# One run of products through both halves of a channel mixer, with the second half's operands prepared early and kept in DRAM

## The chip, the cores and the metric

The kernel runs on one core of a Trainium2 chip. The metric is the device time of one execution in microseconds (us). The core has TensorE (PE: matrix products, from SBUF into PSUM), VectorE (DVE), ScalarE (ACT) and GpSimd (POOL) for elementwise work, and SyncE (SP), whose queue issues nearly all transfers of this kernel. Each engine takes its instructions in order.

## What is computed

The reference is one encoder block on x of 2048 positions by 1024 channels. The change touches the second sub-layer alone, the channel mixer:

```python
h = rms_norm(x, g_pre_ffn[l]) * (1.0 + sc_f) + sh_f
y = conv_ffn(h, w_up[l], w_dw_ffn[l], b_dw_ffn[l], w_down[l])
x = x + gt_f * rms_norm(y, g_post_ffn[l])

def conv_ffn(h, w_up, w_dw, b_dw, w_down):
    u = causal_dwconv(h @ w_up, w_dw, b_dw)      # width 3 over positions
    val, gt = jnp.split(u, 2, axis=-1)           # 2 x 2816 channels
    return (jax.nn.gelu(gt) * val) @ w_down
```

## The kernel before

Data lie channels by positions, in tiles of 128 channels by 512 positions. Numbers are kept accurate by splitting each operand in a high and a low part: a product of two operands is three matmuls (high-high, low-high, high-low).

The channel mixer works in two halves of 1024 positions. A half is a loop of 22 **stages**, one for each block of 128 value channels and 128 gate channels (`n`, `NJ = 22`). The up-projection of a stage is a 2x2 block product in seven products instead of eight: seven **token terms** (B11, T2, T1, B21, T3, T4, B22), which are sums and differences of blocks of h, meet seven weight factors (A11, S2, S1, A12, S3, A22, S4), which are sums and differences of blocks of `w_up`. `sprod` (L1179) issues one such product, 12 matmuls at L1188. The token terms (28 pairs of tiles, two f16 parts each) are made once for each half by `h2prep` (L1119): it loads x from DRAM (`XD`), scales it (L1129), and forms and splits the terms on VectorE and ScalarE. They stay in SBUF for the whole half, in the pool `fh`, which has room for one half's terms.

The weights of each stage are loaded (`upload`, two 512 KB loads to the tile `wst`, of which there are three), combined (`combine`), and split with a power-of-two scale `sw` (`pairV`, `pairA`, `pairB`, `pair4`, all through `wpair`, L288 on ScalarE and L289 on VectorE). The scale comes from the weights' squares: `upsquare` (ScalarE, L259), then `uptable` (L1098), which is a small matmul (L1104), about six small VectorE instructions (L219 to L224) to the power of two, and three more. Squares and tables are made in the first half only; the second half finds `sw` in SBUF.

The order of one stage n, as TensorE sees it, is: on odd n above 2, first the down-projection `down` of the two gated blocks before it (96 matmuls, L1263 to L1265); A11 of n; A22 and S4 of n-1; S2 of n; then, in the first half, the small matmul of `uptable(n+1)`; S1, A12 and S3 of n. `order` chains all of these in the order of the program. `pairV(n+1)`, which makes the weights of the next stage's first product, stands behind A12 of n, and `ready(n+1)` (the loads and squares of the next weights) behind A11 of n. Between the products the results are taken from PSUM to the rows `ub`, convolved (`taps3`, L1241 to L1247), multiplied (L1405) and split into `gh` and `gl`, the operands of `down`, whose results VectorE adds to `y2` (L1273).

Other work is hung under the products with a generator, `under`: each `sprod` takes one step of it. In the first half it is `post(NB - 1)`, the rest of the sub-layer before; in the second half it is `finals` of the first half (mean square, scale, residual, store). Between the halves stands, not hung under anything:

```python
        dw[NG - 1] = [dchunk(C_DN + 4 * (NG - 1) + q) for q in range(4)]
        if half == 0:
            down(NG - 1)
            h2prep(1)
            under = finals()
        else:
            down_final()
```

`dchunk` loads a 256 KB piece of `w_down` into a tile `xt` (four of them in all, which `h2prep` and `finals` use too) and splits it into `whi` and `wlo`. `tc.high_priority(offset=...)` tells the scheduler to place instructions as if they stood that many instructions earlier in the program; a tile that is asked for again is given out when its last reader is done.

The functions that the change touches:

Of the kernel before, what the change touches and what calls it, by code (L numbers as in the profile page):

```python
# [78 lines left out]
def hybrid_block_kernel(ctx: ExitStack, tc: tile.TileContext, xT, vec, bvrow, band, wada, wall, outT):  # L79
# [1007 lines left out]
    hb = {}  # L1087

# [24 lines left out]

    def htile(x, i):
        t = fh.tile([P, 2, 512], F16, name=f"{x}_{i}")
        hb[x, i] = t[:, 0, :], t[:, 1, :]
        return hb[x, i]

    def h2prep(half):  # L1119

        ta = fa.tile([P, 2, 512], F32, name="ta", tag="t0", bufs=1)
        tb = fa.tile([P, 2, 512], F32, name="tb", tag="t1", bufs=1)
        for i in range(4):
            x = {}
            for q, bb in ((0, 0), (0, 1), (1, 1), (1, 0)):
                k = 4 * q + i
                xt = mx.tile([P, 512], F32, name="xt", tag="xt", bufs=4)
                SY.dma_start(out=xt, in_=XD[2 * half + bb][k])
                V.scalar_tensor_tensor(out=xt, in0=xt, scalar=fsc[:, k:k + 1], in1=r2k[2 * half + bb], op0=ALU.mult, op1=ALU.mult)  # L1129
                x[q, bb] = xt  # L1130

# [3 lines left out]
            def direct(name, q, bb):  # L1135
                hi, lo = htile(name, i)
                A.activation(hi, x[q, bb], AF.Identity, bias=shift(q))
                V.scalar_tensor_tensor(out=lo, in0=x[q, bb], scalar=shift(q), in1=hi, op0=ALU.add, op1=ALU.subtract)

            def summed(name, t):  # L1140
                hi, lo = htile(name, i)
                A.activation(hi, t, AF.Identity)
                V.tensor_tensor(out=lo, in0=t, in1=hi, op=ALU.subtract)

            t1, t3, t2, t4 = ta[:, 0, :], ta[:, 1, :], tb[:, 0, :], tb[:, 1, :]
            direct("B11", 0, 0)
# [3 lines left out]
            summed("T2", t2)  # L1150
            summed("T1", t1)
            V.scalar_tensor_tensor(out=t3, in0=x[1, 1], scalar=shift(1), in1=x[0, 1], op0=ALU.add, op1=ALU.subtract)
            direct("B21", 1, 0)
            summed("T3", t3)
            V.scalar_tensor_tensor(out=t4, in0=x[1, 0], scalar=shift(1), in1=t2, op0=ALU.add, op1=ALU.subtract)
            summed("T4", t4)
            direct("B22", 1, 1)
# [13 lines left out]
    h2prep(0)  # L1171
    NG = NJ // 2
    under = post(NB - 1)
# [19 lines left out]
    for half in range(2):  # L1193
        y2, W, U, gt, stg, sums = {}, {}, {}, {}, {}, {}

        def pairs(st, j, tag):

            t = m1.tile([P, 2, 1024], F16, name="up", tag=tag)
            wpair(st, U_UP + 2 * j, (t[:, 0, :], t[:, 1, :]))
            return [(t[:, 0, c:c + 512], t[:, 1, c:c + 512]) for c in (0, 512)]  # L1200

        def combine(j, st, half=half):

            a, g = st
            if j == 0 and half == 0:
                s12 = wp.tile([P, 1024], F32, name="wst", tag="wst", bufs=3)
            else:
                s12 = fr.tile([P, 1024], F32, name="s12", tag="r2k0")
            s4 = fa.tile([P, 512], F32, name="s4", tag="s4", bufs=1)
            s2, s1 = s12[:, 0:512], s12[:, 512:1024]  # L1210
            V.tensor_tensor(out=s1, in0=g[:, 0:512], in1=g[:, 512:1024], op=ALU.add)
            V.tensor_tensor(out=s2, in0=s1, in1=a[:, 0:512], op=ALU.subtract)
            V.tensor_tensor(out=g[:, 0:512], in0=a[:, 0:512], in1=g[:, 0:512], op=ALU.subtract)
            V.tensor_tensor(out=s4, in0=a[:, 512:1024], in1=s2, op=ALU.subtract)  # L1214
            return s12, s4

        def pairV(j):
            W["A11", j], W["A12", j] = pairs(stg[j][0], j, f"yl{j % 2}")

        def pairA(j):  # L1220
            W["S2", j], W["S1", j] = pairs(sums[j][0], j, "yl2")

        def pairB(j):
            W["S3", j], W["A22", j] = pairs(stg[j][1], j, "yl3")

        def pair4(j):
            t = fa.tile([P, 2, 512], F16, name="up4", tag="up4", bufs=1)
            W["S4", j] = t[:, 0, :], t[:, 1, :]
            wpair(sums[j][1], U_UP + 2 * j, W["S4", j])

        def urow(j, part):

            r = fa.tile([P, 1026], F32, name="ub", tag=f"u{part}", bufs=2 - part)
            G.tensor_copy(r[:, 0:2], carry[:, part * NJ + j, :])  # L1234
            return r

        def taps3(j, part, half=half):
            fi, r = part * NJ + j, U.pop((j, part))
            t = fa.tile([P, 1024], F32, name=f"t{part}", tag=f"t{part}", bufs=1)
            f = fws[:, j, part, :]  # L1240
            A.activation(t, r[:, 2:1026], AF.Identity, scale=f[:, 2:3], bias=col("fb", fi))  # L1241
            if half == 0:
                G.tensor_copy(carry[:, fi, :], r[:, 1024:1026])
            V.scalar_tensor_tensor(out=t, in0=r[:, 1:1025], scalar=f[:, 1:2], in1=t, op0=ALU.mult, op1=ALU.add)  # L1244
            V.scalar_tensor_tensor(out=t, in0=r[:, 0:1024], scalar=f[:, 0:1], in1=t, op0=ALU.mult, op1=ALU.add)  # L1245
            if part:
                A.activation(t, t, AF.Gelu_apprx_tanh)  # L1247
            return t

        def down(g, last=False):  # L1250
            w = dw.pop(g)
            for q in range(4):
                wh, wl = w[q]
                for mm in range(2):
                    m = 2 * q + mm
                    for bb in range(2):
                        ps = pr2.tile([P, 512], F32, name="mx")
                        c = slice(bb * 512, (bb + 1) * 512)
                        mms = []
                        for jj in range(2):  # L1260
                            gh, gl = gt[2 * g + jj]
                            a, b = [x[:, (2 * mm + jj) * P:(2 * mm + jj + 1) * P] for x in (wh, wl)]
                            mms.append(T.matmul(ps, a, gh[:, c], start=jj == 0, stop=False))  # L1263
                            T.matmul(ps, b, gh[:, c], start=False, stop=False)  # L1264
                            mms.append(T.matmul(ps, a, gl[:, c], start=False, stop=jj == 1))  # L1265
                        order(mms[0], mms[-1])
                        with tc.high_priority(offset=WPRI // 4):
                            if g == 0:
                                y2[m, bb] = m1.tile([P, 512], F32, name=f"y2_{m}_{bb}", tag=f"{('ym', 'yh')[bb]}{m}")
                                A.activation(y2[m, bb], ps, AF.Identity)  # L1270
                            else:
                                y = y2[m, bb]
                                V.tensor_tensor(out=y, in0=y, in1=ps, op=ALU.add)  # L1273

        def dchunk(i):

            with tc.high_priority(offset=WPRI):
# [15 lines left out]
        def finish(bb, c0, c1, ps, xt, last, half=half, y2=y2):  # L1293
            b = 2 * half + bb
            with tc.high_priority(offset=WPRI):
                r = rstd(ps, mx, 1, after=last, n=c1 - c0)
# [214 lines left out]
```

## Time and profile before

| | us |
|---|---|
| median of 3 runs (2994.25 to 2995.7) | 2994.99 |
| the profiled execution | 2989.23 |
| its span | 2987.4 |
| first-half stages, two and one `down`, from 1922.33 | 64.84 |
| second-half stages, two and one `down`, from 2418.78 | 59.32 |
| last S3 of the first half to the end of the first `down` of the second, 2199.81 to 2359.46 | 159.65 |

The profile times each instruction of one execution from the start of its span. The channel mixer runs from about 1493 us on to the end. Matmuls are pipelined: a row's length of a product (2.75 us for 12 matmuls) overlaps the next one's, and the distance from start to start is what counts. The stretches of the table are cut where TensorE ends a `down` and starts the next A11; 2199.81 is where the last S3 of the first half would be followed by the next product.

### The profile page before, as it was taken

To read this page: it belongs to the slowest core of one execution; us is meant where nothing else is said; L and a number is where in the kernel's file an instruction comes from. 1 tells how busy PE (TensorE), PEld (TensorE's weight loads), DVE (VectorE), ACT (ScalarE), POOL (GpSimd) and SP (SyncE) were. 2 spreads that over 40 slices of the span, in tenths; PEclk is the share of its full clock that TensorE was granted. 3 is DMA by queue.
4 is the path that set the end of the run, shared out by engine and by line. 5 is a ranking of instruction groups with operands and counts; after the bars stand their busy time and mean duration, and the time that the engine had idled before them with its cause. 6 is when DMAs were issued, how large, how long until landed. Compare 5 with 4: busy or idle time off the path is not lost. (4 is left out here: it accounts for less than half of the span.)

```text
span 2987.4 us, 38687 instructions
## 1 busy us (share of the span) xinstructions
PE 2776.3 (93%) x14286; PEld 1616.5 (54%) x14286; DVE 2282.7 (76%) x3360; ACT 1427.9 (48%) x2210; POOL 385.8 (13%) x387
## 2 busy tenths in 40 slices
PE   7999999999899999999879999999986899999996
PEld 3576666654344446556625555555552556556654
DVE  7858677669999575876986766777799677777776
ACT  5745766632312455555666334444455533443344
POOL 2102222200000002221201000101124000000002
PEclk8999999999999999999989999999998999999998
DMA  8657665531312466655641111111124311211121
GB/s 290 202 153 211 200 189 176 170 94 50 106 60 95 166 193 188 215 188 150 190 133 43 54 43 44 49 50 58 52 64 137 93 51 52 61 57 47 53 70 58
DMA packets 221215, 340.17 MB, mean 114 GB/s; under 512 B 52832, under 2 KB 69344, under 8 KB 221024
## 3 DMA queue, kind: packets, MB, share of 16 engines
q1 hardware_dynamic: 221024, 337.68, 36.6%
q8 instruction: 112, 1.84, 0.3%
q14 instruction: 79, 0.65, 0.1%
HBM read 268.40 MB, written 69.21 MB: 113 GB/s over the span
## 5 line engine op out<-in xcount | busy, mean ns | idle before, releaser
L1188 PEld LDWEIGHTS <-up 128*128 128x128 f16 x3696 | 364.8, 100 | 516.5 <-issue 65.2
L1188 PE MATMUL g<-T,up 128*128 128x512 f16 x1584 | 365.8, 381 | 4.0 <-DVE up L289 1.8
L402 PE MATMUL g<-hh,whi 128*128 128x512 f16 x768 | 295.4, 385 | 6.5 <-ACT whi L288 4.2
L1273 DVE TENSOR_TENSOR y<-y,mx 128x512 f32<-128x512 f32 x304 | 207.5, 685 | 120.3 <-PE mx L1265 117.8
L404 PE MATMUL g<-hh,whi 128*128 128x512 f16 x768 | 292.4, 383 | 2.4 <-DVE hh L364 2.0
L403 PE MATMUL g<-hh,wlo 128*128 128x512 f16 x768 | 293.4, 383 | 0.0
L1263 PE MATMUL mx<-gh,whi 128*128 128x512 f32 x672 | 273.3, 407 | 12.2 <-ACT gh L325 10.5
L846 DVE SCALAR_TENSOR_TENSOR a<-ut,vc,a 128x2048 f32<-128x2048 f32 x120 | 279.6, 2348 | 2.1
L1265 PE MATMUL mx<-gl,whi 128*128 128x512 f32 x672 | 269.4, 401 | 8.9 <-DVE gl L326 8.8
L1264 PE MATMUL mx<-gh,wlo 128*128 128x512 f32 x672 | 267.7, 398 | 8.3 <-DVE wlo L326 8.3
L289 DVE SCALAR_TENSOR_TENSOR up<-wst,sw,up 128x1024 f16<-128x1024 f32 x89 | 113.9, 1280 | 151.7 <-ACT up L288 151.7
L1188 PE MATMUL g<-B,up 128*128 128x512 f16 x528 | 141.2, 419 | 48.8 <-DVE up L289 19.9
L1234 POOL COPY ub<-carry 128x2 f32<-128x2 f32 x88 | 97.1, 1105 | 657.1 <-DVE t L1245 560.2
L1263 PEld LDWEIGHTS mx<-gh,whi 128*128 128x128 f32 x672 | 127.5, 190 | 49.7 <-ACT gh L325 15.5
L1265 PEld LDWEIGHTS mx<-gl,whi 128*128 128x128 f32 x672 | 127.3, 189 | 47.3 <-DVE gl L326 17.5
L325 ACT ACTIVATE whi<-xt 128x512 fp32r<-128x512 f32 x88 | 53.9, 625 | 204.8 <-PE mx L1265 203.7
L717 ACT ACTIVATE sx<-sx,st 128x640 f32<-128x640 f32 (+4 forms) x128 | 97.4, 761 | 109.6 <-DVE st L715 88.4
L1264 PEld LDWEIGHTS mx<-gh,wlo 128*128 128x128 f32 x672 | 127.6, 190 | 38.3 <-DVE wlo L326 8.7
L720 DVE SCALAR_TENSOR_TENSOR ph<-sx,ph 128x640 f16<-128x640 f32 (+4 forms) x128 | 94.6, 739 | 65.2 <-POOL ph L719 64.4
L719 POOL TENSOR_SCALAR ph<-sx 128x640 f16<-128x640 f32 (+4 forms) x128 | 89.3, 698 | 411.1 <-ACT sx L717 353.8
L1376 ACT ACTIVATE ub<-g 128x512 f32<-128x512 f32 x44 | 26.3, 597 | 229.9 <-PE g L1188 229.7
L440 ACT ACTIVATE ev<-g,hbias,si 128x512 f32<-128x512 f32 x64 | 49.6, 775 | 173.3 <-PE g L404 149.4
(376 smaller groups left out, 6215.5 us busy)
## 6 DMA issues: line engine op xcount, KB each, us to landing
wst<-in_wall_dram SPq DMA_DIRECT2D x152, 512.0 KB, 3.7
wst<-in_wall_dram SPq DMA_DIRECT2D x144, 256.0 KB, 2.8
xt<-in_wall_dram SPq DMA_DIRECT2D x88, 256.0 KB, 2.7
xt<-in_xT_dram SPq DMA_DIRECT2D x64, 256.0 KB, 4.6
kt<-KD SPq DMA_DIRECT2D x64, 256.0 KB, 4.2
ast<-in_wada_dram SPq DMA_DIRECT2D x64, 256.0 KB, 3.3
GD<-ev SPq DMA_DIRECT2D x64, 256.0 KB, 2.5
xt<-XD SPq DMA_DIRECT2D x48, 256.0 KB, 2.8
```

The source lines that it names most:

```text
L289: V.scalar_tensor_tensor(out=lo, in0=st, scalar=sw[:, u:u + 1], in1=hi, op0=ALU.mult, op1=ALU.subtract)
L402: a = T.matmul(ps, wh, xh, start=(i == 0), stop=False)
L403: T.matmul(ps, wl, xh, start=False, stop=False)
L404: yield a, T.matmul(ps, wh, xl, start=False, stop=(i == KT - 1))
L717: A.activation(sx[:, 0:W], sx[:, 0:W], AF.Exp, scale=-1.0, bias=st, accum_out=sms[h, b][:, t])
L846: V.scalar_tensor_tensor(out=a1, in0=ut[:, k:k + S], scalar=wt[k], in1=a1, op0=ALU.mult, op1=ALU.add)
L1188: mms.append(T.matmul(ps, a[:, c], b, start=not more and i + q == 0, stop=i == 3 and q == 2, skip_group_check=more))
L1234: G.tensor_copy(r[:, 0:2], carry[:, part * NJ + j, :])
L1263: mms.append(T.matmul(ps, a, gh[:, c], start=jj == 0, stop=False))
L1264: T.matmul(ps, b, gh[:, c], start=False, stop=False)
L1265: mms.append(T.matmul(ps, a, gl[:, c], start=False, stop=jj == 1))
L1273: V.tensor_tensor(out=y, in0=y, in1=ps, op=ALU.add)
```

## The change

The two loops become one loop over 44 stages q (`LAST = 43`; the weights are those of `q % NJ`), with these parts:

- `h2prep` is a generator with 12 steps for each of its four channel groups. For the second half it hangs under the first half's products, behind `post`. It makes its terms in tiles of `mx` (`hst`, on the tags `rv` and `rr`, one each) and stores each pair of tiles to DRAM (`HPD`, 28 stores of 256 KB). `use` issues a product, and at q = 21 it loads the term that this product was the last to read (`hload`, four loads of 256 KB for each term, 28 in all) into the same place in `fh`.
- A11 of stage 22 follows S3 of stage 21 at once. `down` of the first half's last two blocks stands at the start of stage 23, as in any odd stage. It now takes the squares and their sum (ScalarE, POOL) as it goes, and `finals` hangs under the products behind it. The gain `Gf` is multiplied in `finish` with the rstd in one VectorE instruction for five of eight tiles, and on ScalarE for three, in place of 16 ScalarE instructions.
- Within a stage, `uptable(n+1)` moves from behind S2 to ahead of it, `pairV(n+1)` from behind A12 to ahead of `combine`, and `ready` from behind A11 of n (for n+1) to the end of n (for n+2).
- At the end, `down(20)` moves from the start of stage 43 to behind the last stage, ahead of `down_final`; the gated block 42 has tiles of its own for this.

```diff
+    HPD = {(x, i): dr.tile([P, 2, 512], F16, name=f"HPD{x}_{i}") for x in TERMS for i in range(4)}
...
+    def hload(x):
+
+        for i in range(4):
+            SY.dma_start(out=htile(x, i), in_=HPD[x, i])
...
+            if half:
+                t1, t2, t3, t4 = [mx.tile([P, 512], F32, name="ht", tag=g, bufs=2) for g in ("acc", "acc", "sq", "sq")]
             x = {}
...
                 x[q, bb] = xt
+                yield
...
+            def term(name, t, sh=None):
+                nonlocal n
+                o = htile(name, i) if half == 0 else mx.tile([P, 2, 512], F16, name="hst", tag=("rv", "rr")[n % 2], bufs=1)
+                n += 1
+                hi, lo = o[:, 0, :], o[:, 1, :]
...
+                if half:
+                    SY.dma_start(out=HPD[name, i], in_=o)
...
-    h2prep(0)
+    run(h2prep(0))
     NG = NJ // 2
-    under = post(NB - 1)
+
+    def rest():
+        yield from post(NB - 1)
+        yield from h2prep(1)
+
+    under = rest()
...
+                    if g == NG - 1:
+                        last = sumsq(y2[half, m, bb], m, accs[bb], G)
+        return [accs, last] if g == NG - 1 else None
...
+            if gained:
+                e.tensor_tensor(out=y, in0=y, in1=r, op=ALU.mult)
+            elif e is V:
+                V.scalar_tensor_tensor(out=y, in0=y, scalar=Gf[:, m:m + 1], in1=r, op0=ALU.mult, op1=ALU.mult)
             else:
...
+                A.activation(y, y, AF.Identity, scale=Gf[:, m:m + 1])
+                G.tensor_tensor(out=y, in0=y, in1=r, op=ALU.mult)
...
+        if q == LAST - 1:
+            gt[q] = [m1.tile([P, 1024], F32R, name="gh", tag=f"yl{q % 2}"), fr.tile([P, 1024], F32R, name="gl", tag="r2k0")]
         else:
...
+            gt[q] = [fa.tile([P, 1024], F32R, name=x, tag=x, bufs=2) for x in ("gh", "gl")]
...
+    def use(ps, w, q, x, more=False):
+        sprod(ps, W.pop((w, q)), x, more)
+        if q == NJ - 1:
+            hload(x)
...
+    ready(1)
+    for n in range(LAST + 2):
+        p = n - 1
+        nxt_ = n + 1 <= LAST
+        if n % 2 and 2 < n < LAST:
+            st = down((n - 3) // 2)
+            if st is not None:
+                under = finals(*st)
+        if n <= LAST:
+            bA[n] = pg.tile([P, 512], F32, name="g")
+            use(bA[n], "A11", n, "B11")
...
+        if n + 1 < NJ:
+            mm = uptable(n + 1, stab)
+            order(mm, mm)
+        if nxt_:
+            pairV(n + 1)
+            sums[n + 1] = combine(n + 1, stg[n + 1])
+        if n:
+            tg = taps3(p, 1)
+        if n <= LAST:
+            use(bA[n], "S2", n, "T2", True)
...
+            if n + 2 <= LAST:
+                ready(n + 2)
+        if n % 2 == 0 and 1 < n < LAST:
+            dchunks((n - 2) // 2)
+    down(2 * NG - 2)
+    dchunks(2 * NG - 1)
+    down_final()
```

## Rows read from the trace of the kernel before

**Rows 1.** The page, parts 1 and 2: busy time by engine; 40 slices of 74.7 us.

```profile
PE 2776.3 (93%) x14286; PEld 1616.5 (54%) x14286; DVE 2282.7 (76%) x3360; ACT 1427.9 (48%) x2210; POOL 385.8 (13%) x387
...
PE   7999999999899999999879999999986899999996
```

**Rows 2.** Busy time by stretch: edges, length, busy (count) by engine, granted clock, DMA.

```profile
1492.68:1576.40 83.72, 61.20 (x241) 25.51 (x240) 75.12 (x136) 53.12 (x72) 6.92 (x8) 0.86 0.39 126
...
1600.18:2181.66 581.48, 550.28 (x2413) 314.67 (x2412) 425.02 (x671) 246.64 (x326) 56.44 (x72) 0.98 0.17 51
...
1922.33:1987.17 64.84, 61.52 (x270) 35.08 (x269) 46.79 (x74) 27.08 (x36) 6.38 (x8) 0.97 0.17 49
...
2199.81:2359.46 159.65, 113.67 (x449) 64.76 (x448) 140.85 (x163) 89.21 (x129) 51.04 (x34) 0.85 0.36 111
...
2418.78:2478.10 59.32, 58.95 (x266) 34.36 (x265) 44.79 (x54) 23.73 (x28) 4.39 (x4) 1.00 0.18 54
```

**Rows 3.** Waits of TensorE, 1600 to 2180 (total us, times, longest).

```profile
PE g L1188 <- DVE up L289: 11.9, 9, 1.3
...
PE mx L1265 <- DVE gl L326: 5.5, 9, 0.6
```

**Rows 4.** Timeline, 1867 to 1884: start, length, engine, line, operation, tiles, idle before.

```profile
1867.87 0.28 PE L1104 MATMUL st<-su,on_d 128*128 128x1 f32 x2
...
1874.52 0.14 DVE L221 TENSOR_SCALAR sw<-pf 128x1 int32<-128x1 int32 x1
...
1876.04 1.13 ACT L288 ACTIVATE up<-wst,sw 128x1024 f16<-128x1024 f32 x1
...
1877.22 0.39 PE L1188 MATMUL g<-B,up 128*128 128x512 f16 x1 [1.29 <-ACT up L288]
...
1878.94 4.24 PE L1188 MATMUL g<-B,up 128*128 128x512 f16 x11 [1.33 <-DVE up L289]
...
1883.01 2.75 PE L1188 MATMUL g<-T,up 128*128 128x512 f16 x12
...
1885.60 2.75 PE L1188 MATMUL D<-B,up 128*128 128x512 f16 x12
```

**Rows 5.** Instructions on the tile `xt`: durations in ns, minimum, median, maximum.

```profile
L1129 DVE SCALAR_TENSOR_TENSOR xt<-xt,fsc,r2k x32: 735/741/1773, 1437.6 to 2266.0; 128x512 f32<-128x512 f32 x32
...
L1138 DVE SCALAR_TENSOR_TENSOR B<-xt,fsc,B x24: 736/742/1833, 1453.0 to 2271.0; 128x512 f16<-128x512 f32 x24
...
L1147 DVE TENSOR_TENSOR ta<-xt x8: 677/678/692, 1451.6 to 2266.6; 128x512 f32<-128x512 f32 x8
```

**Rows 6.** VectorE groups by line, 2206 to 2270.

```profile
L1129 DVE SCALAR_TENSOR_TENSOR xt<-xt,fsc,r2k 128x512 f32<-128x512 f32 x12 | 12.9, 1103 | 0.0
...
L1273 DVE TENSOR_TENSOR y<-y,mx 128x512 f32<-128x512 f32 x16 | 10.8, 677 | 0.4 <-PE mx L1265 0.2
```

**Rows 7.** Waits of TensorE, 2180 to 2345.

```profile
PE g L1188 <- ACT B L1137: 12.1, 2, 9.6
...
PE mx L1263 <- ACT gh L325: 9.3, 1, 9.3
...
PE mx L1264 <- DVE wlo L326: 8.3, 1, 8.3
```

**Rows 8.** VectorE groups by line, 2270 to 2345.

```profile
L1302 DVE TENSOR_TENSOR xt<-xt,y 128x512 f32<-128x512 f32 x10 | 10.2, 1035 | 0.0
...
L1300 DVE TENSOR_TENSOR y<-y,rr 128x512 f32<-128x512 f32 x10 | 9.1, 941 | 0.0
```

**Rows 9.** Waits of TensorE, 2900 to the end.

```profile
PE mx L333 <- ACT gh L325: 6.5, 1, 6.5
```

**Rows 10.** Waits of TensorE, 1490 to 1600.

```profile
PE st L1104 <- DVE su L1102: 6.4, 2, 3.4
```

**Rows 11.** The page, part 5 (ns of one) and part 6 (KB, us to landing).

```profile
L289 DVE SCALAR_TENSOR_TENSOR up<-wst,sw,up 128x1024 f16<-128x1024 f32 x89 | 113.9, 1280 | 151.7 <-ACT up L288 151.7
...
xt<-XD SPq DMA_DIRECT2D x48, 256.0 KB, 2.8
```

More of the change, by code (lines that the diff above doesn't have):

```diff
@@ L1087, in hybrid_block_kernel @@
     hb = {}
+    TERMS = ("B11", "T2", "T1", "B21", "T3", "T4", "B22")
     def upload(j):
@@ new lines, in taps3 @@
+    def taps3(q, part):
+        j = q % NJ
+        fi, r = part * NJ + j, U.pop((q, part))
+        t = fa.tile([P, 1024], F32, name=f"t{part}", tag=f"t{part}", bufs=1)
+        f = fws[:, j, part, :]
+        A.activation(t, r[:, 2:1026], AF.Identity, scale=f[:, 2:3], bias=col("fb", fi))
+        if q < NJ:
+            G.tensor_copy(carry[:, fi, :], r[:, 1024:1026])
+        V.scalar_tensor_tensor(out=t, in0=r[:, 1:1025], scalar=f[:, 1:2], in1=t, op0=ALU.mult, op1=ALU.add)
+        V.scalar_tensor_tensor(out=t, in0=r[:, 0:1024], scalar=f[:, 0:1], in1=t, op0=ALU.mult, op1=ALU.add)
+        if part:
+            A.activation(t, t, AF.Gelu_apprx_tanh)
+        return t
@@ new lines, in dchunk, with dchunks, fstat @@
+    def dchunk(i):
+        with tc.high_priority(offset=WPRI):
+            st = mx.tile([P, 512], F32, name="xt", tag="xt", bufs=4)
+            SY.dma_start(out=st, in_=wall[i])
+        hi = wp.tile([P, 512], F32R, name="whi", tag="whi", bufs=4)
+        lo = wp.tile([P, 512], F32R, name="wlo", tag="wlo", bufs=4)
+        split(hi, lo, st)
+        return hi, lo
+    def dchunks(d):
+        dw[d] = [dchunk(C_DN + 4 * (d % NG) + q) for q in range(4)]
+    def fstat(ps, m, y):
+        sq = mx.tile([P, 512], F32, name="sq", tag="sq", bufs=2)[:, 0:y.shape[-1]]
+        A.activation(sq, y, AF.Square)
+        i = A.activation(y, y, AF.Identity, scale=Gf[:, m:m + 1])
+        return i, lambda: T.matmul(ps, on_d, sq, start=(m == 0), stop=(m == KT - 1))
@@ new lines, in finish @@
+    def finish(b, c0, c1, ps, xt, last, gained):
+        half, bb = divmod(b, 2)
+        with tc.high_priority(offset=WPRI):
+            r = rstd(ps, mx, 1, after=last, n=c1 - c0)
+        for m in range(KT):
+            y = y2[half, m, bb][:, c0:c1]
+            e = G if m in (2, 5, 7) else V
+            if gained:
+                e.tensor_tensor(out=y, in0=y, in1=r, op=ALU.mult)
+            elif e is V:
+                V.scalar_tensor_tensor(out=y, in0=y, scalar=Gf[:, m:m + 1], in1=r, op0=ALU.mult, op1=ALU.mult)
+            else:
+                A.activation(y, y, AF.Identity, scale=Gf[:, m:m + 1])
+                G.tensor_tensor(out=y, in0=y, in1=r, op=ALU.mult)
+            x = xt(m)[:, c0:c1]
+            e.tensor_tensor(out=x, in0=x, in1=y, op=ALU.add)
+            SY.dma_start(out=outT[m, :, b * 512 + c0:b * 512 + c1], in_=x)
+            if m % 4 == 3:
+                yield
```

397 lines of the change are left out of this document (165 added, 232 removed).

## The prediction

> **What bounds the kernel now.** I read the page first: TensorE is busy for 93% of the span, and the slices show it near nine tenths all the way but for dips, one of them three quarters through [rows 1]. So time can only come out of the places where TensorE waits. I then cut the channel mixer into stretches [rows 2]. Two stages of the second half with their down-projection take 59.32 us, of which TensorE is busy 58.95: there nothing is to be had. The same work in the first half takes 64.84. The stretch between the halves takes 159.65 with TensorE busy for 113.67 at a mean granted clock of 0.85, and VectorE busy for 140.85. The beginning of the mixer takes 83.72, with VectorE busy for 75.12.
>
> The waits say why. In the first half TensorE waits nine times for the low part (VectorE, L289) of an `up` weight [rows 3], each time behind a wait for its high part (ScalarE, L288). The timeline shows one of these [rows 4]: the table's matmul is at 1867.87, but the scale is ready only at 1874.52, because the small VectorE instructions queue between the convolution's; the split of the next stage's weights follows at 1876.04, and A11 starts at 1877.22 with a wait of 1.29, then one of 1.33. After that its remaining 11 matmuls run 4.24 us, some 0.385 apart. That is the half clock (1.2 GHz); a product at the full clock (2.4 GHz) takes 2.59 from start to start (1883.01 to 1885.60). Between the halves TensorE waits for terms, for `gh` behind L1405, and for `wlo` [rows 7].
>
> **The boundary.** The stretch of 159.65 us holds 21 products and two `down`. Two second-half periods are 28 products and two `down`: 118.64; less seven products at 2.59 (18.13), the same work at the steady pace is 100.5. The change removes `h2prep` from between the halves and makes the boundary a stage like others: 159.65 - 100.5 = 59.1 can go. What stays is `finals`: its ten multiplications and ten additions on VectorE cost 9.1 + 10.2 [rows 8] and two rstd of four instructions each at 0.68 (by L1147, [rows 5]) 5.4, so 24.7. The multiplications that now take the gain too are scalar_tensor_tensor, 0.74 instead of 0.68 undisturbed [rows 5], which is under 1 us in all. The 16 ScalarE gains fall away to six; ScalarE is busy less than half of a period [rows 2], so that is worth nothing. `finals` falls on stages 23 and 24, whose own VectorE work is 44.8 in 59.3 [rows 2]: 69.5 of work in 59.3 of time leaves 10 over, and the two mean-square matmuls add to it. I take 12 as staying (bounds 2, if it is spread over later stages, and 25, if all of it stands in front of the weights' splits). Gain: 47.
>
> **The first half's weight wait.** From 1600.18 to 2181.66 are nine periods, 581.48 us. At the second half's pace, plus the two tables' matmuls (0.28 long each [rows 4], half of it beside the product behind: 0.28 in all) and a wait of 0.6 for `gl` [rows 3], a period is 60.2, nine are 541.8. So 39.7 us are waits of this kind with their half clock. The change puts the table's matmul one product (2.59) earlier and the small instructions and `pairV(n+1)` ahead of the convolution. The waits in rows 4 are 1.29 + 1.33 = 2.62; the table's 2.59 and the place ahead of the convolution, which now stands between the table and the scale for 6.65 us (1867.87 to 1874.52), cover that. What is late next? The split of `gl`, on which `down` waits already. `pairV` adds 1.28 ahead of it on VectorE [rows 11], but leaves ScalarE's queue ahead of `gh`, where it takes 1.13 [rows 4]; I take these as even (bounds 0 and 1.3 for each of nine periods, 12). Squares and loads stand earlier too, by the freeing of `wst`, so the table should find its sum.
>
> **What is moved in there.** `h2prep(1)` is, for each of four groups, four scalings, three direct low parts and three sums of that kind (0.741 each), and five plain subtractions (0.678): 10 x 0.741 + 5 x 0.678 = 10.8, in all 43.2 us of VectorE [rows 5]. It has 48 steps at 14 a period, so lasts 3.43 periods and asks 12.6 of each. A first-half period has 46.8 of VectorE work already [rows 2]: 59.4 of 60.2. VectorE has been seen to fill 90% of a stretch at best in such a crowd (75.12 of 83.72, and 140.85 of 159.65). At 100% nothing is lost; at 90% a period is 66.0 and 3.43 of them lose 20. I take 92%, a loss of 15 (bounds 0 and 30, the latter with a half clock after each wait). The cover is thus VectorE's idle 18 us of a period; if it is gone, every microsecond counts, as `gl` is late already. ScalarE's eight instructions a group fit in its idle 37 us a period (27.08 of 64.84 busy).
>
> One number here shows why the place matters. Between the halves L1129 takes 1103 ns in the mean, against a median of 741 [rows 5, 6], while POOL is busy for a third of that stretch; L1273, which reads PSUM and SBUF, keeps 677 beside it. In the first half POOL works 6.4 of 64.8 us [rows 2], so I use the medians. The Trainium skill (SBUF — State Buffer, section Who interferes with whom) states that a VectorE instruction with two SBUF inputs contends with a GpSimd one that reads SBUF, over a shared read interface; the rows agree. By that rule `finals`, which keeps POOL and VectorE together, keeps its slowed 24.7, as I have put it, and the moved work would cost 43.2 and not a third more.
>
> The 28 stores and 28 loads are 256 KB each, 2.8 us to landing for such a load [rows 11], and the DMA share of a period is 0.17: no cost. Each store waits on SP for its low part, and behind it in the queue stand the loads of `wst` and `xt`, for which `pairV` and `dchunk` wait; stores that are ready in order cost their issue alone. Each loaded term has a whole stage (over 18 us) until it is read again. I take 0 (bounds 0 and 10).
>
> **The end.** TensorE waits 6.5 for the last `gh` [rows 9], and the matmuls after it run at half clock as in rows 4, some 2 us. `down(20)`, 23 us, now covers this. Gain 9 (bounds 5 and 10).
>
> **The beginning.** TensorE waits twice for the squares' sum, 6.4 in all [rows 10]. With the table ahead of S2, S2 stands behind that wait: at most 2 x 2.59 = 5.2 more. I take 2.6.
>
> **The sum.** -47 - 39.7 + 15 - 9 + 2.6 = -78. The profiled execution is 2989.2, so 2911; the median of the runs is 5.8 above it, so **2917 us**. With `h2prep`, the largest unknown, at its bounds it is 2902 to 2932.
>
> **Rivals.**
> 1. VectorE can't hold it: the loss of `h2prep` and of the later `gl` eats the first half's whole 39.7. For it: 59.4 of 60.2, and a `down` that already waits for `gl`. Against it: most of the first half (7.6 of 11 periods) has no `h2prep`. -47 - 9 + 2.6 = -53: 2941.
> 2. The first half's weight wait stays, as `sw` waits for the squares or the loads and not for its place; then `h2prep` comes on top: -47 + 15 - 9 + 2.6 = -38: 2957. For it: at the beginning the table does wait for the squares [rows 10]. Against it: in rows 4 the table's matmul itself didn't wait.
> 3. All is covered: `finals` and `h2prep` both fit. -57 - 39.7 - 9 + 2.6 = -103: 2892.
> 4. Slower. `h2prep` holds the four `xt` tiles over twelve steps, and `dchunk` needs the same four for every `down`. If a group's tiles come free only after the `down` should start, TensorE stands for the group's chain and a reload. The four groups between the halves took 64 us (2206 to 2270, [rows 6]), 16 each; with 2.8 for the load and the split behind it some 22, so 88 for four groups: -78 + 88 = +10, 3005. It decides from 19.5 a group on. Against it: a group can run ahead on VectorE without TensorE, and `dchunk` has a priority 400 instructions early, about two stages.
>
> **Numbers.** Forecast 0.52, rival 1 0.20, rival 2 0.10, rival 3 0.12, rival 4 0.06. The range from 2890 to 2960 holds the first four, and leaves rival 4 and the tails out. Of no change I can tell 0.2%, 6 us. Faster 0.92, same 0.02, slower 0.06.
>
> **What would show it.** Right: no wait of `g` for `up` L288 or L289 in the first half, periods of 60 to 61 from the tenth stage on, of 63 to 66 before; the boundary without a stretch of half clock, `finals` costing TensorE some 12; the last `down` followed by `down_final` without a wait for `gh`. Wrong: waits of `mx` for `wlo` or `whi` in stages 3 to 9 (rival 4), of `mx` for `gl` of several us (rival 1), of `st` for `su` in every stage (rival 2). The prediction falls if the scheduler orders VectorE otherwise than by the program's places, above all if `h2prep` is drawn into one block.

## The result and the profile after

The changed kernel takes 2965.36 us in the median (2964.62 to 2966.28, four runs) against 2994.76 for the kernel before, run beside it: a ratio of 0.9902, interval 0.9884 to 0.9919. It is faster by 1%, where 2917 us was forecast, with 2890 to 2960 as the range. The span of the profiled execution went from 2987.4 to 2962.8 us.

To see where the 24.6 us come from, I cut both traces at the starts of the `down` calls, numbered from 0: the beginning ends at down(0), the first half's nine periods run from there to down(9), the boundary from down(9) to down(12), the second half to down(19), and the end from there on.

| us | before | after | difference | forecast |
|---|---|---|---|---|
| to the first product of the mixer | 1501.4 | 1505.9 | +4.5 | 0 |
| from there to down(0) | 75.0 | 79.0 | +4.0 | +2.6 |
| down(0) to down(9) | 581.4 | 582.4 | +1.0 | -39.7 + 15 |
| down(9) to down(12) | 237.7 | 209.2 | -28.5 | -47 |
| down(12) to down(19) | 415.2 | 419.2 | +4.0 | 0 |
| down(19) to the end | 176.7 | 167.2 | -9.5 | -9 |

The first row is no effect of the change: in the kernels below, which don't differ there either, this point lies between 1500.6 and 1508.0. The differences are therefore best read by stretch, and small ones of the total with care; the medians of the kernel before, run beside each group of kernels below, lie between 2991.5 and 2994.8 us.

The page of the kernel after, parts 1 and 2, answers to [rows 1]:

```profile
PE 2757.1 (93%) x14286; PEld 1619.7 (55%) x14286; DVE 2271.5 (77%) x3360; ACT 1423.2 (48%) x2199; POOL 375.3 (13%) x387
...
PE   7899999999899999998978998999998899999997
```

The dip of the boundary is shallower; the shares of the engines are what they were. The stretches, by the same view as [rows 2], with edges at the starts of `down`: the first half's nine periods, one of them, the two periods of the boundary, and one of the second half:

```profile
1584.87:2167.25 582.38, 549.15 (x2413) 322.00 (x2413) 445.39 (x710) 273.99 (x371) 45.66 (x71) 0.97 0.23 70
1911.97:1976.50 64.53, 60.52 (x269) 35.47 (x268) 46.30 (x74) 27.01 (x37) 4.69 (x8) 0.97 0.16 49
2230.47:2376.40 145.93, 124.11 (x534) 71.60 (x533) 106.32 (x121) 75.76 (x101) 48.17 (x34) 0.93 0.32 101
2376.40:2436.29 59.89, 58.94 (x267) 34.33 (x265) 45.11 (x55) 23.74 (x29) 4.39 (x4) 1.00 0.19 53
```

TensorE is still busy for only 549.15 of the first half's 582.38 us, and a late period of it, which has no `h2prep`, is as long as before (64.53 against 64.84), though VectorE is busy for 46.30 us of it. So it isn't the moved work that eats the gain. The waits of TensorE in the first half, 1600 to 2160, answer to [rows 3]:

```profile
PE mx L1299 <- ACT whi L325: 29.8, 8, 3.8
PE mx L1300 <- DVE wlo L326: 2.0, 7, 0.4
PE g L1219 <- DVE up L289: 0.7, 1, 0.7
```

The nine waits for `up` are gone but for one of 0.7 us. In their place stand eight waits, one at nearly each `down`, for `whi`, the high part of the down weights (L325 on ScalarE). The timeline at one of them, 1971 to 1980:

```profile
1971.30 0.37 SPq L254 DMA_DIRECT2D wst<-in_wall_dram  x1
...
1973.04 1.06 ACT L325 ACTIVATE gh<-t 128x1024 fp32r<-128x1024 f32 x1 [2.69 <-DVE t L1398]
1974.00 0.58 ACT L1471 ACTIVATE ub<-g 128x512 f32<-128x512 f32 x1
...
1974.78 1.06 ACT L259 ACTIVATE junk<-wst 128x1024 bf16<-128x1024 f32 x1 [0.20 <-DMA wst<-in_wall_dram]
...
1975.83 2.18 ACT L325 ACTIVATE whi<-xt 128x512 fp32r<-128x512 f32 x4
...
1976.50 0.64 PE L1299 MATMUL mx<-gh,whi 128*128 128x512 f32 x1 [3.73 <-ACT whi L325]
...
1978.02 0.63 PE L1301 MATMUL mx<-gl,whi 128*128 128x512 f32 x1
1978.02 0.33 PEld L1299 LDWEIGHTS mx<-gh,whi 128*128 128x128 f32 x1
1978.45 0.63 PE L1299 MATMUL mx<-gh,whi 128*128 128x512 f32 x1
...
1980.61 0.39 PE L1299 MATMUL mx<-gh,whi 128*128 128x512 f32 x1
1980.84 0.39 PE L1300 MATMUL mx<-gh,wlo 128*128 128x512 f32 x1
```

The load of `wst` at 1971.30 is that of the stage after next. Its square (L259, tag `junk`) runs at 1974.78, and only behind it do the four splits of `whi` start, in one row at 1975.83, although ScalarE had room before (2.69 us idle) and their own loads were issued at 1912.55:

```profile
1912.55 2.13 SPq L1318 DMA_DIRECT2D xt<-in_wall_dram  x4
```

TensorE stands 3.73 us for the first of them; then its matmuls are 0.43 us apart, against 0.23 from 1980.6 on: half clock (1.2 GHz) for some 4 us. The mean granted clock from 1976.50 to 1980.60 is 0.58, and 1.00 in the 4 us behind that. The code says why: the diff puts `ready(n + 2)` ahead of `dchunks`, and the squares write their unused output into tiles of the tag `whi`, of which there are four, as many as `dchunks` needs.

The waits of TensorE at the boundary, 2180 to 2345, answer to [rows 7]:

```profile
PE g L1219 <- ACT ub L1471: 11.1, 1, 11.1
PE mx L1300 <- DVE wlo L326: 8.5, 1, 8.5
PE g L1219 <- ACT ub L1430: 1.3, 1, 1.3
```

The waits for terms and for `gh` are gone. The A22 product of stage 23, which adds onto the PSUM tile of S3, waits 11.1 us until S3's result is copied (L1471) into a row of `U`, called its evict below, and down(11) waits 8.5 us for `wlo`. The end, 2870 to 2962, answers to [rows 9]: no wait for `gh` is left.

```profile
PE g L1333 <- ACT sq L1331: 5.8, 6, 3.2
```

### The profile page after: what moved, and what is told of

Same layout as the page of the kernel before. It is cut to its first block, busy times and chain, and to the rows that moved or that the text cites. A ratio compares the mean times of both kernels' runs of the same rounds, so it can differ in the third digit from the quotient of the medians.

```text
span 2962.8 us, 38793 instructions
## 1 busy us (share of the span) xinstructions
PE 2757.1 (93%) x14286; PEld 1619.7 (55%) x14286; DVE 2271.5 (77%) x3360; ACT 1423.2 (48%) x2199; POOL 375.3 (13%) x387
## 4 chain that ended last, share of the span: by engine, by line
PE 33%; DVE 16%; DMA 2%; ACT 2%; issue 2%; POOL 0%; SPq 0%; DVEq 0%; ACTq 0%; POOLq 0%
PE g L1219 10%; PE mx L1301 5%; PE mx L1300 5%; PE mx L1299 5%; PE D L1219 3%; DVE up L289 3%; DVE t L1277 2%; DVE t L1276 2%; PE B L1219 2%; DMA wst<-in_wall_dram 1%; ACT up L288 1%; DVE t L1398 1%; DVE gl L326 1%; PE mx L335 1%; PE mx L333 1%
## 5 line engine op out<-in xcount | busy, mean ns | idle before, releaser
L1265 POOL COPY ub<-carry 128x2 f32<-128x2 f32 x88 | 83.7, 952 | 641.3 <-DVE t L1277 576.0
L325 ACT ACTIVATE whi<-xt 128x512 fp32r<-128x512 f32 x88 | 52.3, 624 | 204.8 <-PE mx L1301 202.0
L1219 PE MATMUL g<-B,up 128*128 128x512 f16 x528 | 124.1, 385 | 14.9 <-ACT up L288 9.4
L402 PEld LDWEIGHTS <-whi 128*128 128x128 f16 x768 | 75.7, 99 | 98.7 <-issue 17.4
```

What stands on the lines that cost most here:

```text
L402: a = T.matmul(ps, wh, xh, start=(i == 0), stop=False)
L1219: mms.append(T.matmul(ps, a[:, c], b, start=not more and i + q == 0, stop=i == 3 and q == 2, skip_group_check=more))
```

## The experiments

In this order: what holds the first half, then the boundary, then the moved work, then what can be had. All were timed against the kernel before.

**1. The squares behind the `down` weights.** `ready(n + 2)` goes behind `dchunks`, so that the squares get their `whi` tiles after them.

```
-            if n + 2 <= LAST:
-                ready(n + 2)
         if n % 2 == 0 and 1 < n < LAST:
             dchunks((n - 2) // 2)
+        if n + 2 <= LAST:
+            ready(n + 2)
```

> One edit to the changed kernel: `ready(n + 2)` stands behind `dchunks` instead of ahead of it, nothing else. Theory S: the first half's new wait (TensorE at `down` for `whi`, 3.7 us and a half clock each period) comes from the weights' squares, whose waste output takes tiles of the tag `whi` ahead of the four pieces of `w_down`. Then the nine periods fall from 64.8 to 60 to 61 us, less what `h2prep` then costs in its three: 2920 to 2935 us. Rival Q: the pieces are late because `h2prep` holds `xt` or VectorE is full; then nothing changes, 2960 to 2968.

2928.41 us, ratio 0.9785 (0.9769 to 0.9802). down(0) to down(9) takes 554.8 instead of 582.4 us, the beginning 74.2 instead of 79.0. The waits of TensorE, 1770 to 2130, are now those for the gates:

```profile
PE mx L1299 <- ACT gh L325: 7.3, 5, 1.6
PE mx L1301 <- DVE gl L326: 3.2, 6, 0.5
```

**2. The squares' output in tiles of its own.** The lines stay where the change put them; only the tag differs.

```
-            wsquare(st[i], ssq[:, u:u + 1], wp.tile([P, 1024], BF16, name="junk", tag="whi", bufs=4))
+            wsquare(st[i], ssq[:, u:u + 1], mx.tile([P, 1024], BF16, name="junk", tag=("rv", "rr")[i], bufs=1))
```

> One edit to the changed kernel: the waste output of the squares goes to tiles of its own (tags `rv` and `rr` of `mx`, which `h2prep` and the rstd use too) instead of `whi`; the order of the program stays. Theory S, in the form that it is the shared tiles: the wait for `whi` goes as when the squares are moved, 2920 to 2940. Rival O: it is the place of the squares in ScalarE's queue alone: the wait stays, 2960 to 2968.

2934.65 us, ratio 0.981 (0.9796 to 0.9825). The first half takes 549.8 us, and no wait for `whi` is left; 9.3 us are lost at the beginning (83.5 from the first product to down(0), against 74.2), where `rv` and `rr` have other users. ScalarE's queue, 1920 to 1985, shows the splits spread over the `down` ahead, each as TensorE frees its tile, a period before they are read:

```profile
1960.88 1.06 ACT L259 ACTIVATE junk<-wst 128x1024 bf16<-128x1024 f32 x1 [0.35 <-DMA wst<-in_wall_dram]
...
1966.09 0.63 ACT L325 ACTIVATE whi<-xt 128x512 fp32r<-128x512 f32 x1 [4.06 <-PE mx L1301]
1971.69 0.63 ACT L325 ACTIVATE whi<-xt 128x512 fp32r<-128x512 f32 x1 [4.97 <-PE mx L1301]
```

With `ready` still ahead of `dchunks` in the program, only the tiles can be the cause: by sharing them the squares push the splits behind themselves.

**3. The old places of the table and of `pairV`**, behind S2 and ahead of S3. The rest as changed.

```
-        if n + 1 < NJ:
-            mm = uptable(n + 1, stab)
-            order(mm, mm)
         if nxt_:
-            pairV(n + 1)
...
+        if n + 1 < NJ:
+            mm = uptable(n + 1, stab)
+            order(mm, mm)
...
+            if nxt_:
+                pairV(n + 1)
```

> The changed kernel with `uptable` behind S2 and `pairV` behind A12 again, where they were before; all else as changed. If their move did what it was to do, the first half's wait for the `up` weight comes back on top of the wait for `whi`: some 4 us in each of nine periods, 2985 to 3005. If the places don't matter: 2960 to 2968. In the second half each `down` should start some 0.5 us earlier if `pairV` ahead of the convolution is what made `gl` later there: 10 periods, 5 us.

3047.82 us, ratio 1.0191 (1.0176 to 1.0206), much slower than expected: with the old places both kinds of wait stand in the first half (667.3 us). TensorE, 1670 to 2180:

```profile
PE mx L1299 <- ACT whi L325: 49.2, 6, 8.3
PE g L1219 <- DVE up L289: 9.3, 7, 1.3
PE g L1219 <- ACT up L288: 9.0, 7, 1.3
```

So the two moves do take away the waits for `up`. The wait for `whi` is longer than in the changed kernel, up to 8.3 us against 3.8, which I hadn't expected and did not trace. The second half is at 415.2 us here, as before, instead of 419.2.

**4. `finals` in blocks of two tiles instead of four** (`if m % 2: yield` in place of `if m % 4 == 3`).

> The changed kernel with a step of `finals` for each two tiles instead of four, so that it spreads over eight products. If the loss behind the boundary (A11 of stage 24 at 13.8 us, the next `down` at 34.2) comes from `finals` standing in one block ahead of the convolution on VectorE, it falls by 8 to 18: 2947 to 2957. If VectorE and POOL simply have too much work in these two stages, it moves but stays: 2960 to 2968.

2964.1 us, ratio 0.9909 (0.9894 to 0.9924): no change. The boundary took 210.0 us; its waits only moved (10.1 for `whi`, 5.2 for the evict of `U`, 3.9 for `wlo`). The next kernels all start from experiment 1 (2928.41 us, boundary 205.8).

**5. All sixteen tiles of `finals` on VectorE.**

```
-            e = G if m in (2, 5, 7) else V
+            e = G if gained and m in (2, 5, 7) else V
```

> Base: the kernel with the squares behind the `down` weights (2928.4 us; its two periods after down(10) 75.9 and 68.8 us, against 59.9 later). Here all sixteen tiles of `finals` are made by VectorE, none by GpSimd. VectorE's own twenty instructions of `finals` took 20.0 us there (the scaling ones 11.5 us for ten, 0.74 us when alone; the adds 8.5 us for ten, 0.68 us when alone), so thirty-two at their undisturbed price are 22.7 us, and its taps beside them get back some 2 us. Theory C, that VectorE is slowed beside GpSimd and that this holds up the row buffer of `U`: VectorE's load stays and the wait for `U`'s evict shrinks, 2917 to 2924 us. Theory V, that it is the amount of VectorE's work in these two periods, wherever it is made: no change, 2925 to 2931 us. Theory G, that GpSimd was a help: 2932 us or more.

2930.02 us, ratio 0.9793 (0.9777 to 0.981): the same as experiment 1. The multiplications and additions of `finals` (instructions of one line: minimum, median, maximum in ns) do go back to their undisturbed length,

```profile
L1345 DVE SCALAR_TENSOR_TENSOR y<-y,Gf,rr x16: 742/744/751, 2228.5 to 2259.6; 128x512 f32<-128x512 f32 x16
...
L1350 DVE TENSOR_TENSOR xt<-xt,y x16: 681/688/693, 2230.4 to 2261.5; 128x512 f32<-128x512 f32 x16
```

but the wait for the evict of `U` is 11.3 us all the same, and the time is that of theory V. VectorE has twelve instructions more here, and these two lines take 22.1 us of it instead of 20.0 in experiment 1: what the undisturbed length gives back, the added instructions take. So giving GpSimd's tiles to VectorE gains nothing. What the lengthening costs by itself, no run separates.

**6. In the second half `pairV` at its old place**, ahead of S3 (`if n + 1 < NJ` at the new place, `>= NJ` at the old).

> Base as above (2928.4 us). In the second half the A11 and A12 weights are again made behind the A12 product, as before the change; the first half keeps the new place. Theory: the new place costs 0.57 us of each period of the second half (59.9 against 59.3), through `gl` that VectorE makes behind that pair; so the seven or eight full periods after down(12) come back to 59.3 us and the whole to 2922 to 2925 us. Rival: in the second half too the pair comes too late for A11 once the squares stand elsewhere: 2930 us or more, with waits for `up`.

2927.75 us, ratio 0.9789 (0.9774 to 0.9803), above the 2922 to 2925 expected. down(12) to down(19) is back at 415.2 us, the 4.0 us that were lost; but down(0) to down(9) and the boundary, which the edit should not touch but at its edge, were 2.9 and 2.3 us longer in the profiled execution, so the median shows nothing.

**7. `finals` without its work.** The output of the first half is the mixer's sums as they are; norm, gain and residual are left out.

```
-            yield from finish(b, 0, 512, meansq(accs[b]), row, last, False)
+            for m in range(KT):
+                SY.dma_start(out=outT[m, :, b * 512:(b + 1) * 512], in_=y2[0, m, b])
...
```

> Base as above (2928.4 us). The first half's `finals` leave out the norm, the gain and the residual: the mixer's sums go to the output as they are. If `finals` alone is what lengthens the boundary, the two periods come to 60 to 62 us each, and the kernel to 2902 to 2907 us. If sums of squares inside down(10), the loads of the laid-aside terms or the clock are a part of it, the periods stay at 65 us or more and the kernel above 2912 us.

2901.74 us, ratio 0.9701 (0.9686 to 0.9715). The boundary takes 180.9 us, 24.9 less. The two periods behind down(10), the view of [rows 2], with `finals` (experiment 1) and without:

```profile
2195.90:2340.60 144.70, 122.84 (x534) 70.65 (x533) 106.21 (x121) 75.91 (x101) 48.24 (x34) 0.94 0.32 102
```

```profile
2190.80:2310.60 119.80, 117.88 (x530) 68.69 (x529) 82.18 (x93) 66.72 (x89) 27.88 (x22) 1.00 0.27 88
```

119.80 us are two second-half periods. All that the boundary still costs is `finals`: it has 24.0 us of work on VectorE (106.21 less 82.18), 20.4 on GpSimd and 9.2 on ScalarE, and costs 24.9 us of time, though VectorE was idle for 38.5 of the 144.70 us. Where this idle time lies shows why. By the same view, without `finals`, the 14 products between down(10) and down(11), then down(11) itself:

```profile
2214.79:2250.72 35.93, 35.93 (x170) 16.30 (x167) 28.96 (x31) 21.43 (x26) 7.61 (x7) 1.00 0.27 85
2250.72:2274.68 23.96, 23.00 (x99) 18.06 (x98) 6.98 (x10) 11.63 (x20) 0.00 (x0) 1.00 0.12 34
```

With `finals` (experiment 1), the same 14 products, then the stretch from the end of the first rstd on:

```profile
2219.64:2271.60 51.96, 39.48 (x173) 17.43 (x171) 46.71 (x50) 26.12 (x33) 23.68 (x17) 0.90 0.57 187
2226.77:2286.62 59.85, 38.94 (x162) 19.02 (x161) 58.94 (x63) 26.00 (x32) 25.72 (x16) 0.86 0.59 193
```

Without `finals`, VectorE has 24.0 us free in this period, but only 7.0 of them ahead of down(11); 17.0 lie within it. With `finals` it gets 17.8 us more to do ahead of down(11), and from 2226.77 until 15 us into down(11) it is full (58.94 of 59.85 us).

**8. Without `h2prep(1)`**, its stores and its loads: the second half works on the first half's terms.

```
-        yield from h2prep(1)
...
-        if q == NJ - 1:
-            hload(x)
```

> Base as above (2928.4 us). The second half's token terms aren't made, stored or loaded: it works on the first half's terms. My prediction priced this work at +15 us (0 to 30) and the stores and loads at 0 (0 to 10). By the periods (those with this work and those without it differ by under 3 us in sum) it is now worth 0 to 4 us: 2924 to 2929 us. If the prediction's price were right it would be 2913 us or less.

2928.78 us, ratio 0.9792 (0.9777 to 0.9807): equal to experiment 1, which has all of this work. down(0) to down(9) takes 556.7 us without it and 554.8 with it. With it VectorE is busy 56.08 us of the 60.00 from 1642 to 1702:

```profile
1642.00:1702.00 60.00, 58.93 (x267) 34.52 (x268) 56.08 (x92) 32.25 (x46) 4.45 (x8) 1.00 0.35 119
```

`h2prep` also fills the time within a `down` that `finals` doesn't reach. In experiment 1, down(1), beside `h2prep`, and down(6), without it:

```profile
1640.05:1665.30 25.25, 23.28 (x99) 17.90 (x98) 24.61 (x38) 7.28 (x11) 0.18 (x1) 1.00 0.30 104
1950.19:1975.41 25.22, 23.30 (x99) 17.98 (x98) 16.48 (x24) 3.85 (x6) 0.18 (x1) 1.00 0.06 21
```

**9 to 12. The order of `finals`.** In 9 its residual rows use the two `sq` tiles instead of the four `xt` tiles, which `dchunk` needs. In 10, besides, the sixteen tiles are put behind fourteen products, none ahead of the first taps. 11 is 10 with the rows in `xt`. 12 is 10 with `pairV` as in 6.

```
-                xt = mx.tile([P, 512], F32, name="xt", tag="xt", bufs=4)
+                xt = mx.tile([P, 512], F32, name="xt", tag="sq", bufs=2)
...
-                under = finals(*st)
+                under = paced(finals(*st), (0, 0, 0, 2, 1, 2, 1, 1, 1, 1, 2, 2, 2, 1))
```

> Base: the kernel with the squares behind the `down` weights (2928.4 us; the two periods after down(10) 75.9 and 68.8 us, of which the run without `finals` gave back all, 59.9 each; TensorE waits there 11.2 us for the S3 evict of `U` and 8.4 us for `wlo`). Here the residual rows of `finals` go into the two `sq` tiles and no longer share the four `xt` tiles with the `down` weights' loads. Theory R, that down(11)'s weights are late because their loads wait for those tiles: the second period comes to 60 to 63 us, the first stays near 76, and the kernel is at 2918 to 2923 us. Theory V, that its splits are late because VectorE is behind with its work: no change, 2925 to 2931 us. With two tiles instead of four the rows could themselves be late: 2932 us or more.

> As the kernel before it, and the sixteen tiles of `finals` are put behind fourteen products one or two at a time, beginning behind the first taps of the period (0, 0, 0, 2, 1, 2, 1 and 1, 1, 1, 2, 2, 2, 1), in place of four blocks of four ahead of and among those taps. VectorE is busy 46 us of an undisturbed period of 59.9 us, and `finals` has 20 to 23 us for it: half of that in each of two periods makes 57 us. Theory O, that the order on VectorE is the cause (a block of `finals` ahead of the taps that free `U`'s row): both waits go, the periods come to 60 to 63 us and the kernel to 2903 to 2912 us. Theory A, that the amount is the cause: VectorE is full, and 2920 us or more remain.

> The same spread of `finals`, but with its rows in the `xt` tiles again. Under theory R down(11)'s weights are now later still (the last row leaves its tile one period later): a wait of 8 us or more at down(11), 2914 to 2925 us. Under theories O and V the tiles don't matter: the same time as the kernel before it within 2 us.

> Squares behind the `down` weights, `finals` spread with its rows in the `sq` tiles, and in the second half the A11 and A12 weights made behind the A12 product again. Seven to nine periods at 59.3 us instead of 59.9: 4 to 5 us less than the run with the first two alone, 2899 to 2908 us if that one is at 2903 to 2912 us.

| | median | ratio | boundary |
|---|---|---|---|
| 9 | 2932.19 | 0.9796 (0.9781 to 0.9811) | 208.0 |
| 10 | 2924.26 | 0.9769 (0.9754 to 0.9783) | 203.8 |
| 11 | 2942.4 | 0.9828 (0.9814 to 0.9843) | 218.4 |
| 12 | 2922.45 | 0.9766 (0.975 to 0.9783) | 203.9 |

The waits of TensorE, 2190 to 2420, in 10 and in 11:

```profile
PE mx L1299 <- ACT gh L325: 9.4, 1, 9.4
...
PE mx L1299 <- ACT y L1306: 4.0, 3, 3.0
...
PE g L1219 <- ACT ub L1461: 0.4, 1, 0.4
```

```profile
PE mx L1299 <- ACT whi L325: 29.3, 1, 29.3
```

In 10 the wait of A22 for the evict of `U`, 11.2 us in experiment 1, is gone; the 0.4 us left are S3's, for the copy of S2's result (L1461). In 9 it has fallen to 0.2, though its edit moves only the rows; but the order on VectorE has changed there as well. The copy that A22 waits for needs the row that two taps (L1276, L1277) read. In experiment 1 five instructions of `finals` stand between these two, and the copy comes behind the second:

```profile
2238.71 1.27 DVE L1276 SCALAR_TENSOR_TENSOR t<-ub,fws,t 128x1024 f32<-128x1024 f32 x1
...
2250.25 2.28 DVE L1277 SCALAR_TENSOR_TENSOR t<-ub,fws,t 128x1024 f32<-128x1024 f32 x1
...
2252.62 0.60 ACT L1471 ACTIVATE ub<-g 128x512 f32<-128x512 f32 x1 [12.02 <-DVE t L1277]
```

In 9 none of them stands there:

```profile
2236.58 1.27 DVE L1276 SCALAR_TENSOR_TENSOR t<-ub,fws,t 128x1024 f32<-128x1024 f32 x1
...
2238.38 1.27 DVE L1277 SCALAR_TENSOR_TENSOR t<-ub,fws,t 128x1024 f32<-128x1024 f32 x1
```

Counted from the start of down(10), the second tap starts at 54.6 us in 1, behind 13 of the 20 instructions that VectorE has of the tiles of `finals`; at 43.6 us in 9, behind 7; and at 35.1 us in 10, behind none. So this wait comes from the order on VectorE, `finals` ahead of the taps that free `U`'s row. But in 10 only 2.0 us of the boundary are won (205.8 to 203.8), as down(11) now waits for `gh`, another instruction behind `finals` on VectorE: the wait went as theory O said, and the time is theory A's. 9 alone trades one wait for the other: VectorE sits 12.1 us for rows that come into two tiles, and down(11) waits 20.2 us for `gh`. Theory R had the second period at 60 to 63 us and the first near 76; they are 82.6 and 64.3. 11 shows the sharing of `xt`: with the rows there, and later than before, down(11)'s weights are 29.3 us late, and the kernel is far above the 2914 to 2925 us of theory R. So theory R names a holder of down(11), but not the only one. 12 has the second half's 415.2 us of 6; its median is 1.8 us below that of 10, where 4 to 5 were expected.

**13 to 15. What holds down(11).** 13 is 12 with four places for the rows: the two `sq` tiles and the halves of `r2k1`. 14 is 13 without GpSimd, 15 is 13 with down(11) behind the S4 product.

> Base: squares behind, `finals` spread, pair late in the second half (2922.45 us; periods after down(10) 65.8 and 76.6 us). Spreading took away the wait for `U`'s evict (11.2 us), but down(11) now waits 9.4 us for `gh` and 4.0 us for ScalarE's copy into `y2`, and VectorE sat 9.5 us for rows that come into two tiles. Here the rows have four places: the two `sq` tiles and the two halves of `r2k1`, which nothing else uses by then. If the rows are what is late (theory R2): the second period comes to 60 to 66 us, the kernel to 2908 to 2914 us. If VectorE's amount beside GpSimd is (theory V): 2919 us or more.

> As the run before it, with all sixteen tiles of `finals` on VectorE. Where GpSimd took six tiles, single VectorE instructions beside it went from 0.74 to 1.7 us and from 1.27 to 2.2 us. With the order and the rows mended, theory C expects this to show now: 2 to 6 us below the run with GpSimd, 2902 to 2911 us. Theory V (the amount alone): equal within 2 us.

> As the run with four rows and GpSimd, and down(11), the first of the second half, stands behind the S4 product of its period instead of ahead of A11: 7.7 us later, so `finals` has three products more to give the `y2` tiles back. If that hand-over of `y2` is what holds down(11): what is left of its wait goes, up to 7 us; 2903 to 2910 us. If `gh` and `gl` (VectorE) are what is late: about the same as that run.

13: 2916.6 us, ratio 0.9741 (0.9728 to 0.9754), the best of the kernels with all of the work, and between the ranges of its two theories; boundary 201.0. 14: 2919.8 us, 0.9748 (0.9735 to 0.9761), no gain from leaving GpSimd out, where theory C had 2902 to 2911. 15: 2928.11 us, 0.9777 (0.9763 to 0.979), slower, above both of its expectations: the wait moved to the A11 ahead of down(11). TensorE, 2190 to 2420, in 13 and in 15:

```profile
PE D L1219 <- DVE ub L1451: 2.8, 1, 2.8
...
PE mx L1299 <- ACT gh L325: 12.7, 1, 12.7
```

```profile
PE g L1219 <- DVE up L289: 19.9, 1, 19.9
```

In 15 it is the low part of an `up` weight that comes late, on VectorE again. The hand-over of `y2` is not what holds down(11) in 13, where no wait for it is left; in 10 and 12 it was 4.0 and 6.6 us (L1306). VectorE in 13, from its first weight split behind down(10) to the end of down(11)'s wait for `gh`, is full:

```profile
2225.59:2274.80 49.21, 33.64 (x144) 14.82 (x141) 48.53 (x51) 28.92 (x31) 19.40 (x14) 0.87 0.47 146
```

## Why the prediction was wrong

The sum had 78 us, and the traces differ by 24.6. The first half falls short of its forecast by 25.7 us, the boundary by 18.5, the second half by 4.0 and the beginning by 1.4.

**The boundary.** That 59.1 us could go was right: without `finals` 56.8 of them did (237.7 to 180.9). The term that failed in size is "I take 12 as staying": 28.3 us stay in the changed kernel (209.2 against 180.9), and 24.9 with the squares moved, about the upper bound of 25. The step behind it that failed is "69.5 of work in 59.3 of time leaves 10 over". It counts VectorE's idle time wherever it lies. In the period from the end of down(10) to the end of down(11), 59.9 us, VectorE has 35.9 us of its own work (experiment 7), as ScalarE makes the copies of down(11); with the 24.0 of `finals` that would just fit. But 17.0 of the 24.0 free us lie within down(11), and `finals` stands ahead of it, where 7.0 are free. The reason that I had put beside the bound of 25, all of it in front of other work, was nearer than the term. So `U`'s row is late (11.1 us), then down(11)'s weights (8.5 us). The first of these is shown to come from the order on VectorE, by experiments 1, 9 and 10. For the second the experiments leave less: the rows' sharing of `xt` with `dchunk` is one holder (11 against 10: 14.6 us), too few places for the rows another (12 against 13, 2.9 us of boundary), and with both mended 12.7 us of a wait for `gh` remain, at the end of a stretch in which VectorE is full. That the amount of work at this place makes these 12.7 us is read from the trace; no run keeps `finals` and takes a part of it out of there. Which order of VectorE and ScalarE would end the wait was not found. Giving GpSimd's tiles to VectorE was tested twice (5, 14) and gains nothing, which leaves the price of the contention itself open. What the prediction took from the Trainium skill (SBUF — State Buffer, section Who interferes with whom), that a VectorE instruction with two SBUF inputs contends with a GpSimd one that reads SBUF, agrees with the lengths of single instructions: the scaling ones of `finals` take 0.737 to 1.795 us beside GpSimd in 1, and 0.742 to 0.751 without it in 5.

**The first half's weight wait.** The step to the waits for `up` was right: they are gone, and experiment 3 brings them back. What failed is my "What is late next? The split of `gl`". What was late next was `whi`. I had read of the moved `ready` only that "squares and loads stand earlier too, by the freeing of `wst`" and did not ask which tiles the squares write and which step they are now ahead of. That took back all: 3.73 us of wait at a `down`, and half clock behind it, gave a period of 64.5 us where 61.5 is had without (experiment 1; by experiment 2 the cause is the shared tiles). It was the mark that I had named for rival 4, but not by its mechanism: `h2prep` and `xt` have no part in it, since periods without `h2prep` have it too. With the cause removed, down(0) to down(9) is 554.8 us, near the 541.8 + 15 of the forecast, and this partly by chance: each late period is 61.5 rather than 60.2 us, with waits for `gh` and `gl` of 1.6 and 0.5, which I did not trace further, and `h2prep` costs nothing.

**What is moved in.** `h2prep` at +15 was wrong, its lower bound of 0 right. I had taken 92% as the most that VectorE holds in a crowd; it held 93% (56.08 of 60.00) with no loss to TensorE, as `h2prep` could also use the time that VectorE has free within a `down`. Rival 1 falls with this. The stores and loads at 0 were right (experiment 8).

**`gl` even.** It was not: `pairV` ahead of the convolution costs 0.57 us of each second-half period, 4.0 in all, by the waits for `gl` of up to 1.0 us; at the old place these are 0.4 at most and the seven periods take 415.2 us, as before (experiment 6; 3 has the 415.2 too). My bounds, 0 to 1.3 a period, held it, but I had set them for the first half alone.

**The end and the beginning.** The end: -9.5 against -9. The beginning: from the first product to down(0) +4.0 against 2.6, but this is the wait of down(0) for `whi` (4.3 us); with the squares behind, the stretch takes 74.2 us against 75.0 before, and the table ahead of S2 costs nothing on balance there.

Rival 2 falls by [rows 3] against the waits after, rival 3 by `finals`, rival 4 by the total and by experiment 1.

## What to carry to other kernels

When a step is moved, list what it writes, scratch output included, and every later step that takes a tile from the same pool: a square whose result nobody reads held the weights of a product here, for some 35 us of the whole (ratios 0.9902 and 0.9785). When work is laid beside other work, ask where in the period the engine's idle time lies and what the work has to stand ahead of, not only what share of the period is idle. And when a wait is taken away, look for the next one in the same period before the gain is counted: here each of three mended waits brought out another.

## What the runs showed that was not expected

VectorE at 93% of a period cost TensorE nothing, while at 73% (106.21 of 144.70 us) 24.9 us were lost: the share of the whole stretch hid that VectorE was full ahead of down(11) and into it (58.94 of 59.85 us), and had most of its idle time in the rest of the `down`s. Beside GpSimd single VectorE instructions of `finals` went from 0.744 us to as much as 1.795, and giving GpSimd's tiles to VectorE still gave no time back. The wait of 3.73 us at a `down` was followed by about 4 us at half clock, so that removing it shortened a late first-half period by about 3 us and, with the other waits for `whi`, nine periods by 27.6.
